# Moving the scan mixer's elementwise products from GpSimd to VectorE, and the rounding of all weights from GpSimd to ScalarE

## The chip, the cores and the metric

One core of a Trainium2 chip. TensorE (PE) multiplies matrices into PSUM, VectorE (DVE), ScalarE (ACT) and GpSimd (POOL) work on tiles of 128 partitions, and SyncE (SP) issues most of the loads. Each engine takes its instructions in the order in which the program lists them. The metric is the device time of one execution in microseconds (us), the median of several runs.

## What is computed

Two layers of a diffusion backbone over 256 context tokens and 512 latent tokens of width 1024. Each layer mixes tokens with four mixers that run side by side (a bidirectional gated recurrence with a decay per channel, called HGRN2; a bidirectional state-space scan; attention over a 2-D neighbourhood; grouped-query attention), merges them with gates, and then runs a SwiGLU network. In the reference the scan works chunk by chunk:

```python
def step(S, inp):
    qc, kc, vc, gc = inp
    b = jnp.cumsum(gc, axis=2)
    decay = jnp.exp(jnp.where(tri, b[:, :, :, None, :] - b[:, :, None, :, :], -jnp.inf))
    scores = jnp.einsum('bhtk,bhsk,bhtsk->bhts', qc, kc, decay)
    o = jnp.einsum('bhts,bhsv->bhtv', scores, vc) + jnp.einsum('bhtk,bhkv->bhtv', qc * jnp.exp(b), S)
    b_end = b[:, :, -1:, :]
    S = S * jnp.exp(b_end[:, :, 0, :])[..., None] + jnp.einsum('bhsk,bhsv->bhkv', kc * jnp.exp(b_end - b), vc)
    return S, o
```

## The kernel before

Every large product is made of three matmuls. A float32 operand is split into a rounded high part and a rest, and `mm3` (lines 240 to 246) adds high·high, high·rest and rest·high in PSUM, so a product of one 128-deep slice is the three lines L244, L245 and L246. Activations are split once per stage (the tile `h`); weights are split each time that they are loaded.

`wload` (line 205) loads one block of weights, at most 128x1056, on SP's queue into `wf` (two buffers), makes the high part `wh` on POOL (L219), and the rest `wl = wf - wh` on DVE (L220). `wh` and `wl` have four buffers each, so a block's high part can be written only once PE is done with the block four before it. `wchunk` (line 224) loads 512 or 1024 rows of some columns, one or two calls of `wload`. There are 288 blocks in the program.

The scan mixer (`hgrn`, line 537) takes 128-token tiles two at a time: three such pairs in layer 0, two in layer 1. First it makes the running sums of the log decays (`aB`, L557) and, for both directions, `aks` = key times decay to the end of the tile (L571 to L575, 128x1536), from which PE makes the states. Then for each pair it builds the scores inside a tile level by level (`LEVELS`, seven of them: distances 64, 32, ... 1). One level is: four differences of running sums on DVE (L632 to L635, 128x256 each), two exponentials on ACT (L637, 128x512), the product with the query `E[0] * q` on POOL (L638, 128x512), two products with the keys on DVE (L640, 128x256 each), 32 small matmuls of 64x64 on PE (L615), and the merge of the result into `D2` (L645 and L647 on ACT for the first two levels, L649 on DVE for the others). After the levels come the diagonal, with `kd` = sum of the keys (L651, POOL), and two products with the query for the part that comes through the states (L666, POOL). The tiles of a level are taken from a ring of eleven buffers named `s`.

PE has other work in the meantime: the gates of the merge. `gate_unit` (line 1182) loads 256 columns of the gate's weights for two units, multiplies, and ACT takes the result out of PSUM (L1190); `fill` places such units between the stages, and the ones of the scan and of both attentions run beside them. The attentions take their softmax on ACT (L922 and L925 in the grouped-query one, L977 in the other), and their scores sit in the PSUM buffers `pq` and `pl` that PE needs for the next ones.

The order of the instructions on each engine is not written out by hand: a scheduler in the tile framework goes through the program with a model of the engines' times and lists each engine's instructions in the order in which it expects them to become ready. It decides where between the other instructions a moved one comes to stand.

Of the kernel before, what the change touches and what calls it, by code (L numbers as in the profile page):

```python
# [16 lines left out]
ALU = mybir.AluOpType  # L17
# [72 lines left out]
def block_kernel(ctx, tc, t, out, dbg=None):  # L90
    nc = tc.nc
# [16 lines left out]
    def nm(s):  # L108
        uid[0] += 1
        return f"{s}_{uid[0]}"  # L110

    def pm():
        return ps.tile([P, 512], F32, tag="pm", name=nm("pm"), bufs=2)
# [4 lines left out]
    def pq():  # L118
        return ps.tile([P, 512], F32, tag="pq", name=nm("pq"), bufs=3)
# [88 lines left out]
    def wload(src, a, b):  # L208

        wf = wt.tile([P, WN], F32, tag="wf", name=nm("wf"), bufs=2)  # L210
        wh = wt.tile([P, WN], F32R, tag="wh", name=nm("wh"), bufs=4)
        wl = wt.tile([P, WN], F32R, tag="wl", name=nm("wl"), bufs=4)
        n = 0
        for s in (src if isinstance(src, list) else [src]):
            k = s.shape[-1]
            nc.sync.dma_start(wf[:, :a * b].rearrange("p (a b) -> p a b", a=a)[:, :, n:n + k], s)
            n += k
        assert n == b
        nc.gpsimd.tensor_scalar(wh[:, :a * b], wf[:, :a * b], 1.0, 0.0, op0=ALU.mult, op1=ALU.add)  # L219
        nc.vector.tensor_tensor(wl[:, :a * b], wf[:, :a * b], wh[:, :a * b].bitcast(F32), op=ALU.subtract)  # L220
        return (wh[:, :a * b].rearrange("p (a b) -> p a b", a=a),
                wl[:, :a * b].rearrange("p (a b) -> p a b", a=a))
# [216 lines left out]
    def mixing(l, h, hpool, W0):  # L439
# [9 lines left out]
        with tc.tile_pool(name=f"mx{l}", bufs=1, reuse_waits="tile") as mp:  # L449
            GB = 1552  # L450

            def g6(name, dt=F32):
                return mp.tile([P, GB], dt, tag="g", name=nm(name), bufs=12)


            def s2(shape):

                n = int(np.prod(shape[1:]))
                tl = mp.tile([P, 512], F32, tag="s", name=nm("s"), bufs=11)[:, :n]
                if len(shape) == 2:  # L460
                    return tl
                names = ["a", "b", "c", "d"][:len(shape) - 1]
                return tl.rearrange(f"p ({' '.join(names)}) -> p {' '.join(names)}", **dict(zip(names, shape[1:])))
# [4 lines left out]
            def tu(tl):  # L468
                return tl[:, :1536].rearrange("p (i u s) -> p i u s", i=6, u=2)

            def au(tl):
                return tl[:, :1536].rearrange("p (a s) -> p a s", a=12)
# [64 lines left out]
            def hgrn(q, kf, kb, v):  # L537
# [28 lines left out]
                for d, B, kk in ((0, Bf, kf), (1, Bb, kb)):  # L566
                    ks = g6("aks")
                    ksa = au(ks)
                    end = B[:, :, 128:129].to_broadcast([P, 12, P])
                    if d == 0:  # L570
                        nc.vector.tensor_tensor(ksa, end, B[:, :, 1:129], op=ALU.subtract)  # L571
                        nc.scalar.activation(ksa, ksa, AF.Exp)
                    else:
                        nc.scalar.activation(ksa, B[:, :, 0:128], AF.Exp)
                    nc.gpsimd.tensor_tensor(ksa, ksa, au(kk), op=ALU.mult)  # L575
                    order = [0, 1, 2, 3, 4] if d == 0 else [1, 0, 5, 4, 3]
                    kT = au(g6("akT"))
                    for i4 in range(3):
                        po = pm()
                        for m in range(4):  # L580
                            nc.tensor.transpose(po[:, m * P:(m + 1) * P], ksa[:, i4 * 4 + m, :], ident)
                        nc.scalar.copy(kT[:, i4 * 4:i4 * 4 + 4, :].rearrange("p a s -> p (a s)"), po)
                    St = g6("aS")
                    S4 = tu(St)
                    nc.gpsimd.memset(St[:, :1536], 0.0)
                    nxt = order[1:] + [5 if d == 0 else 2]
                    for n, i in enumerate(order):
                        po = pm()
                        for u in range(2):
                            mm(po[:, u * P:(u + 1) * P], kT[:, 2 * i + u, :], v3[:, i, u * P:(u + 1) * P], start=True, stop=True)  # L590
                        for u in range(2):
                            for hh in range(2):
                                sl = slice(hh * 64, hh * 64 + 64)
                                dst = S4[sl, nxt[n], u, sl]
                                src = po[sl, u * P + hh * 64:u * P + hh * 64 + 64]
                                if n == 0:
                                    nc.vector.tensor_copy(dst, src)
                                else:
                                    nc.vector.scalar_tensor_tensor(dst, S4[sl, i, u, sl], dec[sl, d, 2 * i + u:2 * i + u + 1],
                                                                   src, op0=ALU.mult, op1=ALU.add)  # L600
                    S.append(S4)
                o = g6("ao")
                for i2 in range(i0, TI, 2):
                    a1 = 2 * i2
# [13 lines left out]
                    def block(x, b, off=0):  # L618
                        return x[b * 64:b * 64 + 64, :, (b ^ off) * 64:(b ^ off) * 64 + 64]
                    for li, hlf in enumerate(LEVELS):  # L620
                        E = [s2([P, 4, P]) for _ in range(2)]
                        nb = 64 // hlf

                        def vw(ap):
                            return ap.rearrange("p a (n w s) -> p a n w s", w=2, s=hlf)
                        Eq, Ek = vw(E[0]), vw(E[1])
                        fi, bi = vw(Bf[:, a1:a1 + 4, 1:129]), vw(Bb[:, a1:a1 + 4, 0:128])
                        fx = vw(Bf[:, a1:a1 + 4, 0:128])
                        sh = [P, 4, nb, hlf]
                        fm, bm = fx[:, :, :, 1, 0:1].to_broadcast(sh), bi[:, :, :, 1, 0:1].to_broadcast(sh)  # L630
                        tt = nc.vector.tensor_tensor
                        tt(Eq[:, :, :, 1], fi[:, :, :, 1], fm, op=ALU.subtract)  # L632
                        tt(Eq[:, :, :, 0], bm, bi[:, :, :, 0], op=ALU.subtract)  # L633
                        tt(Ek[:, :, :, 0], fm, fi[:, :, :, 0], op=ALU.subtract)
                        tt(Ek[:, :, :, 1], bi[:, :, :, 1], bm, op=ALU.subtract)  # L635
                        for e_ in E:
                            nc.scalar.activation(e_, e_, AF.Exp)  # L637
                        nc.gpsimd.tensor_tensor(E[0], E[0], au(q)[:, a1:a1 + 4], op=ALU.mult)  # L638
                        for w_, kk in ((0, kf), (1, kb)):
                            nc.vector.tensor_tensor(Ek[:, :, :, w_], Ek[:, :, :, w_], vw(au(kk)[:, a1:a1 + 4])[:, :, :, w_], op=ALU.mult)  # L640
                        pr = scores([pm(), pm()] if li % 2 else [pq(), pq()], E[1], E[0], li == 0)
                        for hh in range(2):
                            if li == 0:
                                for b in range(2):
                                    nc.scalar.copy(block(sc[hh], b, 1), pr[hh][b * 64:b * 64 + 64])  # L645
                            elif li == 1:
                                nc.scalar.copy(D2[:, hh], pr[hh])  # L647
                            else:
                                nc.vector.copy_predicated(D2[:, hh], masks[:, li - 2:li - 1, :].to_broadcast([P, 4, 64]), pr[hh])  # L649
                    kd = s2([P, 4, P])  # L650
                    nc.gpsimd.tensor_tensor(kd, au(kf)[:, a1:a1 + 4], au(kb)[:, a1:a1 + 4], op=ALU.add)  # L651
                    pr = scores([pm(), pm()], kd, au(q)[:, a1:a1 + 4])
                    for hh in range(2):
                        nc.vector.copy_predicated(D2[:, hh], masks[:, 5:6, :].to_broadcast([P, 4, 64]), pr[hh])
# [4 lines left out]
                    for d, B in ((0, Bf), (1, Bb)):  # L659
                        e = s2([P, 4, P])  # L660
                        if d == 0:
                            nc.scalar.activation(e, B[:, a1:a1 + 4, 1:129], AF.Exp)
                        else:
                            nc.vector.tensor_tensor(e, B[:, a1:a1 + 4, 128:129].to_broadcast([P, 4, P]), B[:, a1:a1 + 4, 0:128], op=ALU.subtract)
                            nc.scalar.activation(e, e, AF.Exp)
                        nc.gpsimd.tensor_tensor(e, e, au(q)[:, a1:a1 + 4], op=ALU.mult)  # L666
                        qs.append(e)

                    for i in (i2, i2 + 1):
# [746 lines left out]
    for l in range(DEPTH):  # L1416
# [7 lines left out]
        with tc.tile_pool(name=f"ff{l}", bufs=1, reuse_waits="tile") as fp:  # L1424
# [68 lines left out]
            for pi_, (k0, nk) in enumerate(parts):  # L1493
                a = new_h(hpool)
# [82 lines left out]
```

## Time and profile before

| | before |
|---|---|
| median of 3 runs | 2589.57 us (2587.47 to 2589.83) |
| the profiled execution | 2589.94 us, of which the span of the profile is 2587.9 us |
| PE busy | 2479.7 us (96% of the span) |
| weight loads into PE (PEld) busy | 2116.2 us (82%) |
| DVE busy | 1404.5 us (54%) |
| POOL busy | 824.7 us (32%) |
| ACT busy | 556.1 us (21%) |
| TensorE's granted clock, mean | 0.987 of full |

A row of a view of the profile names the line of the kernel, the engine, the operation, and `out<-in` with the tiles' names. `x35` is a count. In a group's row the busy time and the mean duration of one instruction in ns come first, then the idle time of that engine just before these instructions and which instruction ended it. In the windows view each stretch (us from the start of the span) has its length and then the busy time of every engine, with the number of its instructions in brackets, the granted clock of TensorE as a share of full speed, the share of the DMA engines and GB/s.

### The profile page before, as it was taken

The page shows a single profiled execution, that of the slowest core. Times are in us where ns is not written, and L with a number is a line of the kernel's source. Part 1 is how long each engine was busy: PE and PEld are TensorE (multiplying, and loading weights), DVE is VectorE, ACT ScalarE, POOL GpSimd, SP SyncE. Part 2 cuts the span into 40 slices and gives each one's busy share as a digit, 9 for nine tenths or more (in the row PEclk, how much of TensorE's full clock was granted, in tenths as well). Part 3 has the DMA queues.
Part 4 walks back from the last instruction along what each step waited for, and adds up shares of the span by engine and source line. Part 5 has one row for each costly group of instructions (what it writes and reads, how often), then busy time and mean ns, then how long its engine had stood idle before and what let it go on. Part 6 is the DMA issues. An engine that isn't in the chain of part 4 may idle for free.

```text
span 2587.9 us, 41771 instructions
## 1 busy us (share of the span) xinstructions
PE 2479.7 (96%) x17088; PEld 2116.2 (82%) x17088; DVE 1404.5 (54%) x2646; ACT 556.1 (21%) x1147; POOL 824.7 (32%) x866
## 2 busy tenths in 40 slices
PE   7898899999999999999999999989999999999998
PEld 5777778889778988898998987767877678898987
DVE  4467666446447662343333464868566666443335
ACT  3233332232321141101001033224132311200010
POOL 2233343112114351111141262434223255322324
PEclk9999999999999999999999999999999999999999
DMA  7443113212226454212122164321323255433232
GB/s 244 123 148 124 47 42 89 85 58 70 90 88 210 153 165 127 73 52 64 60 64 66 58 196 136 119 79 50 102 66 107 74 185 176 123 98 98 90 97 76
DMA packets 251938, 269.56 MB, mean 104 GB/s; under 512 B 14971, under 2 KB 219875, under 8 KB 251747
## 3 DMA queue, kind: packets, MB, share of 16 engines
q1 hardware_dynamic: 236867, 238.69, 29.7%
q10 hardware_dynamic: 14880, 28.21, 3.0%
q8 instruction: 134, 2.20, 0.3%
q14 instruction: 57, 0.47, 0.1%
HBM read 238.28 MB, written 26.48 MB: 102 GB/s over the span
## 4 chain that ended last, share of the span: by engine, by line
PE 77%; DVE 10%; POOL 4%; DMA 3%; issue 3%; ACT 2%; SPq 1%; POOLq 0%; ACTq 0%; DVEq 0%
PE pl L244 16%; PE pl L246 15%; PE pl L245 15%; PE pq L245 6%; PE pq L246 6%; PE pq L244 6%; DVE wl L220 2%; DMA wa<-in_ada_w_dram 1%; PE po L311 1%; PE po L954 1%; DVE s L640 1%; DVE s L1243 1%; PE pm L942 1%; POOL wh L219 1%; DVE s L633 1%
## 5 line engine op out<-in xcount | busy, mean ns | idle before, releaser
L219 POOL TENSOR_SCALAR wh<-wf 128x1024 fp32r<-128x1024 f32 (+2 forms) x288 | 332.5, 1155 | 1084.5 <-PE pq L245 475.5
L244 PE MATMUL pl<-h,wh 128*128 128x512 f32 (+1 forms) x1720 | 625.3, 364 | 5.9 <-ACT s L925 1.9
L246 PE MATMUL pl<-h,wl 128*128 128x512 f32 (+1 forms) x1720 | 619.8, 361 | 5.4 <-DVE wl L220 5.4
L245 PE MATMUL pl<-h,wh 128*128 128x512 f32 (+1 forms) x1720 | 620.2, 361 | 0.2 <-DVE h L429 0.2
L220 DVE TENSOR_TENSOR wl<-wf,wh 128x1024 fp32r<-128x1024 f32 (+2 forms) x288 | 403.5, 1406 | 356.9 <-POOL wh L219 353.4
L244 PEld LDWEIGHTS pl<-h,wh 128*128 128x128 f32 x1720 | 327.5, 190 | 71.6 <-issue 17.8
L246 PEld LDWEIGHTS pl<-h,wl 128*128 128x128 f32 x1720 | 327.5, 190 | 61.7 <-issue 8.7
L245 PEld LDWEIGHTS pl<-h,wh 128*128 128x128 f32 x1720 | 327.2, 190 | 51.6 <-issue 7.1
L244 PE MATMUL pl<-wh,h 128*128 128x256 f32 (+1 forms) x1048 | 298.4, 285 | 3.7 <-DVE tmpo L1263 2.2
L245 PE MATMUL pl<-wl,h 128*128 128x256 f32 (+1 forms) x1048 | 297.5, 284 | 1.5 <-DVE wl L220 1.5
L246 PE MATMUL pl<-wh,h 128*128 128x256 f32 (+1 forms) x1048 | 297.1, 284 | 0.0
L244 PE MATMUL pq<-h,wh 128*128 128x256 f32 (+1 forms) x680 | 219.3, 323 | 1.1 <-POOL wh L219 1.1
L246 PE MATMUL pq<-h,wl 128*128 128x256 f32 (+1 forms) x680 | 218.7, 322 | 0.6 <-DVE wl L220 0.6
L245 PE MATMUL pq<-h,wh 128*128 128x256 f32 (+1 forms) x680 | 218.2, 321 | 0.0
L244 PEld LDWEIGHTS pl<-wh,h 128*128 128x128 f32 x1048 | 199.0, 190 | 9.3 <-DVE tmpo L1263 3.7
L245 PEld LDWEIGHTS pl<-wl,h 128*128 128x128 f32 x1048 | 198.8, 190 | 6.4 <-issue 4.0
L246 PEld LDWEIGHTS pl<-wh,h 128*128 128x128 f32 x1048 | 199.1, 190 | 3.2 <-issue 2.9
L245 PE MATMUL pq<-wl,h 128*128 128x256 f32 x600 | 169.1, 282 | 0.0
L244 PE MATMUL pq<-wh,h 128*128 128x256 f32 x600 | 169.0, 282 | 0.0
L246 PE MATMUL pq<-wh,h 128*128 128x256 f32 x600 | 169.0, 282 | 0.0
L244 PEld LDWEIGHTS pq<-h,wh 128*128 128x128 f32 x680 | 127.9, 188 | 15.4 <-issue 2.5
L245 PEld LDWEIGHTS pq<-h,wh 128*128 128x128 f32 x680 | 128.1, 188 | 12.4 <-issue 0.7
(420 smaller groups left out, 3798.1 us busy)
## 6 DMA issues: line engine op xcount, KB each, us to landing
wf<-in_w_in_dram SPq DMA_DIRECT2D x120, 512.0 KB, 3.7
wa<-in_ada_w_dram SPq DMA_DIRECT2D x96, 512.0 KB, 3.9
wf<-in_ffn_w_up_dram SPq DMA_DIRECT2D x176, 256.0 KB, 3.1
wf<-in_ffn_w_down_dram SPq DMA_DIRECT2D x32, 512.0 KB, 3.3
gsp<-gs ACTq DMA_DIRECT2D x32, 384.0 KB, 2.9
gld<-gsp SPq DMA_DIRECT2D x16, 768.0 KB, 4.6
wf<-in_w_branch_dram SPq DMA_DIRECT2D x16, 512.0 KB, 3.3
wf<-in_w_out_dram SPq DMA_DIRECT2D x16, 512.0 KB, 3.3
```

Of the source, the lines that this page charges most:

```text
L219: nc.gpsimd.tensor_scalar(wh[:, :a * b], wf[:, :a * b], 1.0, 0.0, op0=ALU.mult, op1=ALU.add)
L220: nc.vector.tensor_tensor(wl[:, :a * b], wf[:, :a * b], wh[:, :a * b].bitcast(F32), op=ALU.subtract)
L244: mm(po, ah, bh, start=(k == 0), stop=False)
L245: mm(po, ah, bl, start=False, stop=False)
L246: mm(po, al, bh, start=False, stop=(k == n - 1))
L311: mm(po[32 * j:32 * j + 32, :], cT[:, k].rearrange("p r s -> p (r s)"), wf[:, j * 256:(j + 1) * 256], start=(k == 0), stop=(k == KT - 1))
L633: tt(Eq[:, :, :, 0], bm, bi[:, :, :, 0], op=ALU.subtract)
L640: nc.vector.tensor_tensor(Ek[:, :, :, w_], Ek[:, :, :, w_], vw(au(kk)[:, a1:a1 + 4])[:, :, :, w_], op=ALU.mult)
L942: nc.tensor.transpose(pt[:, (2 * k + j) * P:(2 * k + j + 1) * P], x, ident)
L954: mm(po[hh * 64:hh * 64 + 64, :], va(hh, k), PT[hh][k], start=(k == 0), stop=(k == nk - 1))
L1243: nc.vector.scalar_tensor_tensor(tq, sg[:, n % 2, g[0]:g[1]], 1.0, po, op0=ALU.add, op1=ALU.mult)
```

## The change

Three kinds of instruction leave POOL. The rounding of a weight block to its high part (L219, 288 times) goes to ACT, as a copy. The scan mixer's products and sums L575 (4 times, 128x1536), L638 (35 times), L651 (5 times) and L666 (10 times, all 128x512) go to DVE. What is computed stays the same, and so do the loads and the number of buffers. POOL keeps the additions of the merge and the residuals, the small steps of the norms, the rounding of activations, and its part in the state-space scan and the attentions.

```diff
@@ wload
-        nc.gpsimd.tensor_scalar(wh[:, :a * b], wf[:, :a * b], 1.0, 0.0, op0=ALU.mult, op1=ALU.add)
+        nc.scalar.copy(wh[:, :a * b], wf[:, :a * b])
         nc.vector.tensor_tensor(wl[:, :a * b], wf[:, :a * b], wh[:, :a * b].bitcast(F32), op=ALU.subtract)
@@ hgrn
-                    nc.gpsimd.tensor_tensor(ksa, ksa, au(kk), op=ALU.mult)
+                    nc.vector.tensor_tensor(ksa, ksa, au(kk), op=ALU.mult)
...
-                        nc.gpsimd.tensor_tensor(E[0], E[0], au(q)[:, a1:a1 + 4], op=ALU.mult)
+                        tt(E[0], E[0], au(q)[:, a1:a1 + 4], op=ALU.mult)
...
-                    nc.gpsimd.tensor_tensor(kd, au(kf)[:, a1:a1 + 4], au(kb)[:, a1:a1 + 4], op=ALU.add)
+                    nc.vector.tensor_tensor(kd, au(kf)[:, a1:a1 + 4], au(kb)[:, a1:a1 + 4], op=ALU.add)
...
-                        nc.gpsimd.tensor_tensor(e, e, au(q)[:, a1:a1 + 4], op=ALU.mult)
+                        nc.vector.tensor_tensor(e, e, au(q)[:, a1:a1 + 4], op=ALU.mult)
```

The scheduler places the moved instructions. On DVE, in the first pair of tiles of layer 0's scan (the tiles `s` are the levels' operands, `aB` the running sums, `aq`, `akf`, `akb` query and keys, `wl` the rest of a weight block), a piece of the difference between the two orders:

```order
 L634 TENSOR_TENSOR s_1389<-aB_1103 128x64x4
 L635 TENSOR_TENSOR s_1389<-aB_1120 128x64x4
-L220 TENSOR_TENSOR wl_2449<-wf_2447,wh_2448 128x1024
+L638 TENSOR_TENSOR s_1326<-s_1326,aq_612 128x512
 L632 TENSOR_TENSOR s_1419<-aB_1103 128x128x2
 L633 TENSOR_TENSOR s_1419<-aB_1120 128x128x2
 L634 TENSOR_TENSOR s_1420<-aB_1103 128x128x2
 L635 TENSOR_TENSOR s_1420<-aB_1120 128x128x2
+L220 TENSOR_TENSOR wl_2449<-wf_2447,wh_2448 128x1024
 L640 TENSOR_TENSOR s_1327<-s_1327,akf_613 128x16x16
 L640 TENSOR_TENSOR s_1327<-s_1327,akb_614 128x16x16
+L638 TENSOR_TENSOR s_1357<-s_1357,aq_612 128x512
```

The product with the query, which was not on this engine, now stands between the differences of a later level and the products with the keys.

On ACT, in layer 1's grouped-query attention (`ats` and `atm` are the softmax's sums and maxima, `pq`, `pl`, `pm` PSUM buffers, `gs` a gate unit's result on its way out of PSUM):

```order
 L922 ACTIVATE s_19022,ats_19019<-pq_19016,atm_19018 128x256
 L925 ACTIVATE s_19054,ats_19019<-pq_19046,atm_19018 128x512
+L219 CAST wh_19440<-wf_19439 128x1024
 L947 COPY s_18895<-pm_18949 128x512
 L925 ACTIVATE s_19060,ats_19021<-pl_19047,atm_19020 128x512
+L219 CAST wh_19446<-wf_19445 128x1024
 L1190 ACTIVATE gs_19125<-pl_19126 128x512
 L1191 DMA gsp_14512<-gs_19125 128x512
```

The two roundings of a gate block now stand between an exponential of one score block, the copy of the transposed probabilities (L947) and the next exponential, and ahead of the gate unit that is the last one to read the block four before.

## Rows read from the trace of the kernel before

**Rows 1.** The page's part 1: busy time, share of the span and instructions of each engine.
```profile
PE 2479.7 (96%) x17088; PEld 2116.2 (82%) x17088; DVE 1404.5 (54%) x2646; ACT 556.1 (21%) x1147; POOL 824.7 (32%) x866
```
**Rows 2.** Windows: scan, attentions (layer 0); scan, attentions, start of the merge (layer 1).
```profile
97.00:291.00 194.00, 170.74 (x1709) 137.14 (x1709) 138.94 (x267) 65.02 (x125) 74.18 (x60) 0.92 0.37 121
455.00:777.00 322.00, 319.40 (x2023) 261.22 (x2022) 163.41 (x444) 86.23 (x242) 65.06 (x82) 1.00 0.24 78
1585.00:1747.00 162.00, 144.49 (x1234) 118.74 (x1233) 117.88 (x214) 51.58 (x97) 66.38 (x50) 0.97 0.32 101
1844.00:2070.00 226.00, 219.74 (x1304) 172.05 (x1303) 144.91 (x395) 64.28 (x173) 60.21 (x65) 0.98 0.27 85
2102.00:2167.00 65.00, 61.41 (x339) 52.48 (x339) 49.95 (x63) 8.66 (x14) 47.24 (x32) 0.97 0.68 220
```
**Rows 3.** Waits of PE over the whole span: us in total, times, longest.
```profile
PE pq L615 <- DVE s L640: 14.2, 8, 4.4
...
PE pq L615 <- DVE s L649: 10.1, 4, 4.7
PE pq L1168 <- ACT s L925: 6.3, 3, 3.9
...
PE pm L615 <- DVE s L649: 4.8, 3, 2.8
```
**Rows 4.** Timeline of DVE in layer 0's scan: start, duration (us), instruction.
```profile
257.75 0.42 DVE L632 TENSOR_TENSOR s<-aB 128x256 f32<-128x256 f32 x1
258.09 1.54 DVE L633 TENSOR_TENSOR s<-aB 128x256 f32<-128x256 f32 x1
```
**Rows 5.** Timeline of POOL in the same stretch.
```profile
257.92 1.43 POOL L638 TENSOR_TENSOR s<-s,aq 128x512 f32<-128x512 f32 x1 [2.68 <-ACT s L637]
```
**Rows 6.** DVE's groups by shape: the levels' two-input instructions.
```profile
L640 DVE TENSOR_TENSOR s<-s,akb 128x256 f32<-128x256 f32 x35 | 30.4, 869 | 0.0
L640 DVE TENSOR_TENSOR s<-s,akf 128x256 f32<-128x256 f32 x35 | 29.0, 828 | 17.5 <-ACT s L637 17.3
...
L633 DVE TENSOR_TENSOR s<-aB 128x256 f32<-128x256 f32 x35 | 27.3, 781 | 0.0
...
L632 DVE TENSOR_TENSOR s<-aB 128x256 f32<-128x256 f32 x35 | 21.8, 623 | 2.0 <-PE pm L615 2.0
```
**Rows 7.** DVE's groups by shape: two inputs of 512 and of 1536 elements.
```profile
L854 DVE TENSOR_TENSOR s<-s,s 128x512 f32<-128x512 f32 x10 | 6.9, 688 | 4.0 <-ACT s L853 3.9
...
L571 DVE TENSOR_TENSOR aks<-aB 128x1536 f32<-128x1536 f32 x2 | 3.5, 1730 | 0.0
```
**Rows 8.** POOL's groups by shape: two of the scan's products.
```profile
L638 POOL TENSOR_TENSOR s<-s,aq 128x512 f32<-128x512 f32 x35 | 52.2, 1495 | 52.2 <-ACT s L637 46.3 <-issue 5.8
...
L575 POOL TENSOR_TENSOR aks<-aks,akf 128x1536 f32<-128x1536 f32 x2 | 8.8, 4395 | 8.9 <-ACT aks L572 8.9
```
**Rows 9.** The weights' rest on DVE: its group, and its durations (min/median/max, ns).
```profile
L220 DVE TENSOR_TENSOR wl<-wf,wh 128x1024 fp32r<-128x1024 f32 (+2 forms) x288 | 403.5, 1406 | 356.9 <-POOL wh L219 353.4
...
L220 DVE TENSOR_TENSOR wl<-wf,wh x288: 941/1226/4449, 19.3 to 2559.5; 128x1024 fp32r<-128x1024 f32 x142, 128x1056 fp32r<-128x1056 f32 x2
```
**Rows 10.** What POOL waited for ahead of the weights' rounding L219 (us, times).
```profile
  PE pq L245: 475.5, 88
```
**Rows 11.** ACT's groups by shape: the roundings that it does before, two sizes.
```profile
L1509 ACT CAST h<-sg 128x512 fp32r<-128x512 f32 x40 | 24.8, 621 | 232.6 <-DVE sg L1507 232.6
...
L1509 ACT CAST h<-sg 128x256 fp32r<-128x256 f32 x30 | 12.1, 407 | 83.8 <-DVE sg L1507 83.8
```
**Rows 12.** Windows of line L219 alone: length, POOL's busy time and count, clock, DMA.
```profile
97.00:291.00 194.00, 16.63 (x14) 0.92 0.37 121
455.00:777.00 322.00, 29.01 (x26) 1.00 0.24 78
1585.00:1747.00 162.00, 20.33 (x18) 0.97 0.32 101
1844.00:2070.00 226.00, 28.70 (x24) 0.98 0.27 85
```

## The prediction

> **What bounds the kernel now.** I read the busy shares first. PE is busy for 2479.7 us of a span of 2587.9 us and no other engine comes near [rows 1], so whatever this change saves or costs has to show in the 108.2 us in which PE stands still, or in TensorE's clock. None of the moved instructions is on PE, and relief for POOL, busy a third of the span, is no gain by itself.
>
> So the next view is the windows, cut by stage: where does PE stand still? In the two scan stretches it loses 194.0 - 170.7 = 23.3 us (layer 0) and 162.0 - 144.5 = 17.5 us (layer 1), 40.8 us together; in the attentions 2.6 + 6.3 = 8.9 us; at the start of layer 1's merge 3.6 us [rows 2]. The same rows show the granted clock: 0.92 and 0.97 in the scans, 1.00 in layer 0's attentions (1.00 is 2.4 GHz; a mean below it says that a part of the stretch ran at 1.2 GHz). Against full speed that is 0.08 x 194 = 15.5 us and 0.03 x 162 = 4.9 us, 20.4 us in all, and it is lost in the stretches where PE pauses and then runs small matmuls.
>
> The third view is what PE waits for. The scan's small matmuls wait 14.2 + 10.1 + 4.8 = 29.1 us for DVE, for the products with the keys and for the merge of a level's scores [rows 3]. DVE is the late one there: it is busy 139 of 194 us and 118 of 162 us [rows 2].
>
> The fourth view is the timeline inside a level, and it is what this prediction rests on. A difference of running sums takes 0.42 us; the next one, equal in size, takes 1.54 us, and just then POOL runs its product of 1.43 us that began at 257.92 us [rows 4, 5]. It ends at 259.63 us, 0.28 us after POOL's end at 259.35. The reader should see that DVE's "busy" time in the scan is partly time in which it stands behind POOL. The groups show the size of it: equal instructions average 869, 828, 781 and 623 ns in place of 420 [rows 6].
>
> **The change, part by part.** The sum is made against the profiled execution's own 2589.9 us, which is 0.4 us above the median of the three runs.
>
> *Products onto DVE (scan).* Added: 35 + 10 + 5 = 50 of 128x512. The nearest row on DVE with two inputs is 0.688 us [rows 7], so 34.4 us. Removed: with POOL's product gone, the four groups of 35 fall to about 420 ns: 35 x (449 + 408 + 361 + 203) ns = 49.7 us [rows 4, 6]. The four products of 128x1536 go from 4.40 us on POOL to 1.73 us on DVE [rows 7, 8]. During such a POOL product DVE's two-input work stands anyway, so I count the two for which rows show the price, 2 x 2.67 = 5.3 us, and leave the other two at zero.
>
> *Rounding onto ACT, as DVE sees it.* The rest `wl` averages 1.406 us against a median of 1.226 [rows 9]; in the scans there are 14 + 18 = 32 blocks [rows 12], so 32 x 0.18 = 5.8 us less. In the other stages this saves DVE time that PE does not wait for.
>
> DVE's chain in the two scans becomes 34.4 - 49.7 - 5.3 - 5.8 = -26.4 us, that is shorter. What of it does PE get? At most all 26.4; if only the part of PE's idle time counts that names this chain, 29.1 of 40.8, it is 18.8. I take 22, between them, because the gate units that fill PE cannot also be late. The clock's 20.4 us should come back in the same share, 22 / 40.8, which is 11 us. No row shows how the clock answers to fewer pauses; the ends are 0 and 20.4 us.
>
> *Rounding onto ACT, as ACT sees it.* From 621 ns for 512 and 407 ns for 256 elements, ACT adds 214 ns per 256, so a block of 1024 costs it 0.621 + 2 x 0.214 = 1.05 us [rows 11]. For 288 blocks that is some 300 us, and ACT goes from 556 to about 856 us, a third of the span. By throughput that is covered. The covers that could break are two. In the scans ACT's exponentials stand between DVE's differences and the products: 32 blocks x 1.05 = 33.6 us if each delayed the chain, 0 if none did. ACT is busy 65 of 194 us there [rows 2] and several levels are in flight, so I count one block in eight, 4 us. In the attentions there are 26 + 24 = 50 blocks, in 25 pairs [rows 12]: 52.5 us if each of them held PE, 0 if none did. The nearest row is PE's own wait for an exponential there, 6.3 us in three waits [rows 3]; one more block in each of the three is 3.2 us, which I take.
>
> What is queued behind a waiting rounding matters more than its length. POOL waited 475.5 us in 88 places, 5.4 us each, for PE to finish with an older block [rows 10]. On POOL almost nothing stood behind it. On ACT the copy of the probabilities and the next exponential do, as the second piece of the order shows. On SP's queue only a few loads swap places with a neighbour, and a `wf` buffer is given back when the rest is made, so the loads come about when they came.
>
> *Merge.* At its start POOL is busy 47 of 65 us and DVE 50, and PE loses 3.6 us [rows 2]. POOL's roundings go away there: between 0 and 3.6 us, I take 2. The start, the norms and the end keep their POOL steps, and I count nothing.
>
> Sum: -22 - 11 + 4 + 3.2 - 2 = -27.8 us, so 2589.9 - 27.8 = 2562.1; for the median that is **2562 us**. The terms' own ends (18.8, no clock and the ACT costs doubled; 26.4, all of the clock and no ACT cost; the merge's 2 in both) put this case between 2583 and 2541 us.
>
> The Trainium skill, in Perfetto Trace Analysis, section Optimizing Scalar/DVE Operations, says that GpSimd and DVE share an SBUF read port, "so offloading operations between those two might not help". The trace agrees on the sharing (the 1.54 us beside the 1.43 us), but the rule taken as a verdict speaks against moving the products at all. By it the scan would stay as it is and the time would be that of the third rival below.
>
> **The rivals.**
>
> *More than that.* The whole idle time of the scans vanishes with the clock's loss and the merge's: 40.8 + 20.4 + 3.6 = 64.8 us, 2525 us. For it: all the waits named for the scan's matmuls are for DVE [rows 3], and nothing that PE does in the scans is added. Against it: DVE stays busy for two thirds of the scan, and its exponentials now share ACT with roundings. Chance 0.16.
>
> *Slower: roundings hold up the attention.* Place: ACT in both attentions, where a rounding that waits for PE stands ahead of an exponential whose scores hold a PSUM buffer. Price: if each of the 25 pairs costs PE the pair's own 2.1 us, that is 52.5 in place of 3.2 us, and 2562 + 49 = 2611 us. It decides from (27.8 + 3.2) / 25 = 1.24 us of PE per pair on. For it: the 5.4 us waits and the new order. Against it: the scheduler lists by expected readiness, PE has gate units to run, and PE loses only 8.9 us in 548 us of attention now. Chance 0.14.
>
> *No change: one queue's delay for another's.* The roundings stand ahead of the scan's exponentials so often (33.6 us at most) that they eat the 26.4 us; merge and attention leave -2 + 3.2, 2591 us. Against it is ACT's low share. Chance 0.13.
>
> *The change does not do what it says.* DVE's long instructions have another cause, so that DVE gets 34.4 + 4 x 1.73 = 41.3 us and loses nothing; in the share 29.1 / 40.8 PE loses 29 us more, 2619 us. Rows 4 and 5 speak plainly against it. Chance 0.02.
>
> **How the numbers follow.** The forecast has the rest, 0.55, and its own range is 2541 to 2583. A measurement of this kernel can tell 0.2% (5.2 us) from no change, so faster means below 2584.4 and slower above 2594.8. Faster: 0.55 + 0.16 and 0.02 of the third rival's spread, 0.73. Slower: 0.14 + 0.02 and 0.01 of that spread, 0.17. The same: 0.10. For 8 in 10 the range goes from 2535 (it leaves out half of the first rival, 0.08) to 2594 (it leaves out most of the slower cases, 0.12).
>
> **What would show it.** Right: in the scan stretches the levels' L632, L633 and L640 average near 420 ns, L638 on DVE near 0.69 us, PE's waits of L615 for DVE fall from 29 us to under 10, the clock there rises above 0.95, and L220 averages near 1.23 us everywhere. The roundings on ACT take 1.05 us. Wrong: L633 or L640 stay above 600 ns (then POOL was not the cause); PE's waits for L925, L922 or L977 grow beyond 20 us (the slower rival); waits of the scan's PE matmuls name ACT's L637 (the no-change rival). The prediction fails as a whole if PE's idle time in the two scans does not fall by at least a quarter.

## The result, and the profile after

The changed kernel takes 2549.66 us (median of four runs, 2548.04 to 2552.92), the kernel before on the same chip 2589.70 us (2587.47 to 2590.23). The ratio is 0.985, with a 95% interval of 0.9836 to 0.9864. That is 40 us less, where 28 were forecast; the time lies in the forecast's own range of 2541 to 2583. The profiled execution has a span of 2548.6 us, 39.3 us less than before.

The page's part 1 of the changed kernel:

```profile
PE 2475.3 (97%) x17088; PEld 2114.5 (83%) x17088; DVE 1315.8 (52%) x2700; ACT 842.7 (33%) x1437; POOL 393.2 (15%) x524
```

Against [rows 1]: PE runs the same 17088 matmuls and stands still for 73.3 us in place of 108.2. DVE has 54 instructions more and is busy 88.7 us less. That is the first thing to see: work was added to an engine, and its busy time fell.

DVE's groups by shape, the levels' instructions (mean ns after the comma):

```profile
L638 DVE TENSOR_TENSOR s<-s,aq 128x512 f32<-128x512 f32 x35 | 24.0, 685 | 7.8 <-ACT s L637 7.7
...
L633 DVE TENSOR_TENSOR s<-aB 128x256 f32<-128x256 f32 x35 | 15.1, 430 | 0.0
L632 DVE TENSOR_TENSOR s<-aB 128x256 f32<-128x256 f32 x35 | 15.0, 427 | 4.1 <-PE pm L615 3.1 <-PE pm L676 1.0
...
L640 DVE TENSOR_TENSOR s<-s,akf 128x256 f32<-128x256 f32 x35 | 14.7, 419 | 1.0 <-ACT s L637 1.0
L640 DVE TENSOR_TENSOR s<-s,akb 128x256 f32<-128x256 f32 x35 | 14.7, 419 | 0.0
...
L575 DVE TENSOR_TENSOR aks<-aks,akb 128x1536 f32<-128x1536 f32 x2 | 3.5, 1753 | 2.3 <-ACT aks L574 2.3
```

The four groups of [rows 6] are at 419 to 430 ns, the level of the one undisturbed instruction in [rows 4]. The product with the query costs 0.685 us on DVE where it cost 1.495 on POOL [rows 8], and L575 1.75 where it cost 4.40.

PE's waits over the whole span:

```profile
PE pq L1168 <- ACT s L925: 7.6, 3, 3.9
...
PE pm L615 <- DVE s L649: 4.4, 3, 3.4
...
PE pq L615 <- DVE s L640: 3.1, 2, 1.6
```

The scan's small matmuls wait 7.5 us for DVE, where it was 29.1 in the rows shown [rows 3] (30.8 with a wait of 1.7 us for L640 that stands further down in that view).

The same work moves to other times, so stretches are compared between the same instructions in both kernels. For the two scans the windows go from L557 to L808 (a transposition of the state-space scan): in layer 0 from the first of the one to the first of the other, in layer 1 from the last to the last. Before:

```profile
105.00:321.00 216.00, 192.74 (x1806) 155.10 (x1805) 150.64 (x280) 74.31 (x139) 80.07 (x70) 0.93 0.32 104
1606.00:1792.00 186.00, 169.47 (x1326) 139.93 (x1326) 143.84 (x221) 64.70 (x115) 81.70 (x71) 0.97 0.29 91
```

and after:

```profile
102.00:299.00 197.00, 187.24 (x1805) 150.70 (x1804) 135.06 (x313) 91.15 (x156) 10.60 (x24) 0.97 0.36 115
1584.00:1756.00 172.00, 168.99 (x1328) 138.92 (x1327) 125.74 (x244) 84.71 (x135) 13.12 (x26) 0.99 0.32 99
```

PE does the same number of matmuls, but for one, in 369 us in place of 402. Of the 33 us, 27 are idle time (39.8 to 12.8) and 6 are busy time, with a higher granted clock. Elsewhere, from the first instruction of a stage to the first of the next: 3.2 us less before the first scan, 6.2 us more in layer 0's grouped-query attention (208.5 to 214.7 us, L1110 to L1243), 2.8 less in its merge and output product (L1243 to L1505), 3.6 less from there to the last L557 of layer 1, 0.6 less in layer 1's grouped-query attention, 2.6 less in its merge and output product, and 0.2 or less in every other stage. That makes 39.3.

The weights' rounding and rest, from part 5 of the page:

```profile
L220 DVE TENSOR_TENSOR wl<-wf,wh 128x1024 fp32r<-128x1024 f32 (+2 forms) x288 | 368.6, 1284 | 347.0 <-ACT wh L219 346.2
L219 ACT CAST wh<-wf 128x1024 fp32r<-128x1024 f32 (+2 forms) x288 | 298.6, 1037 | 529.3 <-PE pq L246 233.9
```

The rounding waits for PE on ACT as it did on POOL [rows 10]: ACT stands idle 529.3 us ahead of these instructions, most of it for PE, and in most stages this costs nothing. The rest is at 1284 ns, 122 less than in [rows 9].

### The profile page after: what moved, and what is told of

Its sections match the earlier page's. It is cut to its first block, busy times and chain, and to the rows that moved or that the text cites. A ratio compares the mean times of both kernels' runs of the same rounds, so it can differ in the third digit from the quotient of the medians.

```text
span 2548.6 us, 41600 instructions
## 1 busy us (share of the span) xinstructions
PE 2475.3 (97%) x17088; PEld 2114.5 (83%) x17088; DVE 1315.8 (52%) x2700; ACT 842.7 (33%) x1437; POOL 393.2 (15%) x524
## 4 chain that ended last, share of the span: by engine, by line
PE 84%; DVE 6%; DMA 3%; POOL 2%; ACT 2%; issue 2%; SPq 1%; POOLq 0%; ACTq 0%; DVEq 0%
PE pl L244 17%; PE pl L245 17%; PE pl L246 17%; PE pq L244 7%; PE pq L245 7%; PE pq L246 7%; DMA wa<-in_ada_w_dram 2%; PE po L311 1%; PE po L954 1%; DVE wl L220 1%; PE pm L942 1%; PE pq L1168 1%; DVE s L1243 1%; PE po L1001 1%; PE pq L1072 1%
## 5 line engine op out<-in xcount | busy, mean ns | idle before, releaser
L220 DVE TENSOR_TENSOR wl<-wf,wh 128x1024 fp32r<-128x1024 f32 (+2 forms) x288 | 368.6, 1284 | 347.0 <-ACT wh L219 346.2
L219 ACT CAST wh<-wf 128x1024 fp32r<-128x1024 f32 (+2 forms) x288 | 298.6, 1037 | 529.3 <-PE pq L246 233.9
L1267 POOL TENSOR_TENSOR x<-x,tmpo 128x256 f32<-128x256 f32 x100 | 90.3, 904 | 895.6 <-DVE tmpo L1263 885.0
L245 PEld LDWEIGHTS pq<-h,wh 128*128 128x128 f32 x680 | 128.6, 189 | 14.3 <-issue 1.9
```

The source lines that it names most:

```text
L219: nc.scalar.copy(wh[:, :a * b], wf[:, :a * b])
L245: mm(po, ah, bl, start=False, stop=False)
L1267: nc.gpsimd.tensor_tensor(X[t_][:, cs], X[t_][:, cs], tmp, op=ALU.add)
```

## The experiments

Theory: an instruction of DVE with two inputs stands still while POOL reads, so the work taken from POOL gives DVE more than it costs. Rivals: the gain is the rounding's alone, or the new order's.

**Each half alone.** First the products on DVE, with the rounding left on POOL:

```diff
-        nc.scalar.copy(wh[:, :a * b], wf[:, :a * b])
+        nc.gpsimd.tensor_scalar(wh[:, :a * b], wf[:, :a * b], 1.0, 0.0, op0=ALU.mult, op1=ALU.add)
```

> Only the scan's products move to DVE; the weights are still rounded by POOL. Theory A (in the scan POOL's products stop DVE, and that is most of the gain): the prediction's own terms for the products, 34.4 - 49.7 - 5.3 = -20.6 us of DVE's chain, of which PE gets about 17 with about 8 us of clock: 2564 us, between 2558 and 2572. DVE's L633 and L640 fall below 550 ns on average but not to 420, since POOL's roundings still fall among them. Rival B (most of the gain comes from the roundings that leave POOL): 2580 us or more.

Measured: 2562.98 us (2560.89 to 2569.88) against 2589.13, ratio 0.9902 (0.9886 to 0.9919). Then the rounding on ACT, with the products left on POOL (the kernel before with the first line of the change alone):

> Only the rounding of the weights moves to ACT; the scan's products stay on POOL. Theory A: the changed kernel gained 40 us and the products alone should give about 25, so 15 are left: 2575 us, between 2568 and 2586. L220 falls to about 1.25 us outside the scans; L633 and L640 stay near 800 ns inside them. Rival B: 2565 us or less, and the two parts alone sum to the 40 us with the larger share here.

Measured: 2576.91 us (2571.14 to 2579.37), ratio 0.9946 (0.9929 to 0.9962). The halves give 26.2 and 12.2 us, together 38.4 of the 40. DVE's groups show how they share the stall. With POOL's rounding only (the first kernel; its L633 averages 460 ns):

```profile
L634 DVE TENSOR_TENSOR s<-aB 128x256 f32<-128x256 f32 x35 | 17.1, 489 | 0.2 <-PE pm L676 0.2
...
L640 DVE TENSOR_TENSOR s<-s,akf 128x256 f32<-128x256 f32 x35 | 15.5, 444 | 0.8 <-ACT s L637 0.7
```

With POOL's products only (the second; its L633 averages 523 ns, where the expectation had about 800):

```profile
L638 POOL TENSOR_TENSOR s<-s,aq 128x512 f32<-128x512 f32 x35 | 74.7, 2150 | 109.8 <-ACT s L637 99.8 <-PE pl L246 5.2 <-PE pm L679 4.7
...
L640 DVE TENSOR_TENSOR s<-s,akf 128x256 f32<-128x256 f32 x35 | 28.5, 815 | 11.0 <-ACT s L637 10.7
L640 DVE TENSOR_TENSOR s<-s,akb 128x256 f32<-128x256 f32 x35 | 24.4, 696 | 0.0
L632 DVE TENSOR_TENSOR s<-aB 128x256 f32<-128x256 f32 x35 | 20.6, 588 | 1.2 <-PE pm L615 1.2
```

Most of the stall is the products', as forecast, and a smaller part the rounding's. The stall goes both ways, and the mean of 2150 ns hides how (shortest, median and longest in ns):

```profile
L638 POOL TENSOR_TENSOR s<-s,aq x35: 1268/1470/7785, 119.6 to 1712.1; 128x512 f32<-128x512 f32 x35
```

The median is 1470 ns, but four of the 35 products take 5.9 to 7.8 us. Each of these four stands beside 12 to 20 of DVE's two-input instructions that run back to back at their usual length, 0.42 us for 128x256, and it ends 1.15 to 1.18 us after the last of them.

**POOL's reading, put back.** The changed kernel, where POOL makes one more product of the same size in each level, into a tile that nobody reads:

```diff
+                        xt_ = s2([P, 4, P])
+                        nc.gpsimd.tensor_tensor(xt_, E[0], au(q)[:, a1:a1 + 4], op=ALU.mult)
```

> The changed kernel, and beside each of the 35 products on DVE POOL makes the same product once more into a tile of the ring that nobody reads. Nothing waits for it except the ring of eleven buffers. Theory A (POOL at work stops DVE's two-input instructions): DVE stands some 1.1 us in each level again, 35 x 1.1 = 38 us, and also does the products itself: the gain of the products is lost and more, 2575 to 2605 us, L633 or L640 averaging over 600 ns. Rival C (the product is simply sooner done on DVE, 0.69 in place of 1.43 us, and nothing stands): 2550 us, at most 2556, with L633 and L640 near 420 ns.

and, in its place, work for POOL of about the same length that reads nothing:

```diff
+                        xt_ = s2([P, 4, P])
+                        for _ in range(3):
+                            nc.gpsimd.memset(xt_, 0.0)
```

> As the run with the unused product, but POOL only fills that tile with zeros, three times per level, so that it is busy about as long (a fill of 1536 elements took 1.38 us) and the ring is as full, but reads nothing. If what stops DVE is that POOL reads from the same memory, this costs only what the fuller ring costs: 2550 to 2562 us, L633 and L640 near 420 ns. If any work on POOL stops DVE, it costs as much as the unused product. The difference of the two runs is the price of POOL's reading; the difference of this one to the changed kernel (2550) is the ring's.

Measured: 2560.82 us (2559.09 to 2569.54) with the product and 2541.55 (2535.01 to 2543.95) with the memsets. The first lies between the ranges of its theory and its rival: a part of the products' gain is lost, 11 us, not all of it. The second is under its range. DVE's products with the keys and differences with the unread product:

```profile
L642 DVE TENSOR_TENSOR s<-s,akb 128x256 f32<-128x256 f32 x35 | 30.5, 871 | 0.0
...
L642 DVE TENSOR_TENSOR s<-s,akf 128x256 f32<-128x256 f32 x35 | 20.6, 590 | 0.2 <-ACT s L637 0.2
...
L632 DVE TENSOR_TENSOR s<-aB 128x256 f32<-128x256 f32 x35 | 16.4, 468 | 0.1
```

and with the memsets:

```profile
L641 POOL MEMSET s<- 128x512 f32 x105 | 53.1, 524 | 165.8 <-PE pq L615 150.6 <-PE pm L682 5.3 <-PE pm L679 5.3
...
L632 DVE TENSOR_TENSOR s<-aB 128x256 f32<-128x256 f32 x35 | 15.0, 429 | 9.0 <-PE pm L615 6.4 <-PE pm L679 2.4
...
L643 DVE TENSOR_TENSOR s<-s,akf 128x256 f32<-128x256 f32 x35 | 14.8, 422 | 1.6 <-ACT s L637 1.5
L643 DVE TENSOR_TENSOR s<-s,akb 128x256 f32<-128x256 f32 x35 | 14.7, 421 | 0.0
```

The group that runs just after POOL's start pays: 871 ns with reads, 421 with writes of the same size. The two engines' timelines laid side by side say the same of every kernel. Of the levels' 210 instructions of 128x256 on DVE (L632 to L635 and L640 in the kernel before), so many take over 0.5 us, and so much longer than 0.42 us do the 210 take together:

```
kernel                               over 0.5 us   over 0.42 us each, together
before                                   62            51.9 us
products on DVE alone                    18             6.3
rounding on ACT alone                    45            40.2
changed, product nobody reads            35            25.0
changed, three memsets per level         12             2.2
changed                                   7             1.1
```

Every one of the long ones overlaps an instruction of POOL that reads: a product, a rounding or, in all of the last two rows, a copy of a score block (L656). In the memset kernel 48 instructions run beside a memset and nothing else of POOL, and none of them takes over 0.5 us. So it is POOL's reading that stops DVE, not POOL being busy. The 19 us between the two kernels are not all the stall's, though, since their orders differ (below). The Trainium skill, in SBUF — State Buffer, section SBUF: two separate sides, says that a DVE instruction with two SBUF inputs contends only against a GpSimd instruction that reads SBUF. These two runs agree with it. That the memsets would be 8 us faster than the changed kernel itself was not expected. Two questions were left: these 8 us, and the 6 us lost in layer 0's attention.

**The attention's roundings, back on POOL.** A flag is true while the program's text is in the 2-D and the grouped-query attention of a layer and in the gate units that are left after them (the lines that set it are not shown):

```diff
-        nc.scalar.copy(wh[:, :a * b], wf[:, :a * b])
+        if att[0]:
+            nc.gpsimd.tensor_scalar(wh[:, :a * b], wf[:, :a * b], 1.0, 0.0, op0=ALU.mult, op1=ALU.add)
+        else:
+            nc.scalar.copy(wh[:, :a * b], wf[:, :a * b])
```

> The changed kernel, but the blocks loaded while the two attention stages of a layer run are rounded on POOL again. Theory (there ACT's 1.05 us roundings stand ahead of the exponentials and copies that TensorE waits for: layer 0's second attention took 214 us with them and 208 without): that stretch goes back to 208 us, TensorE's wait for L925 goes, and the time falls to about 2544 (2541 to 2547). Rival (the 6 us come from the order of the matmuls or a short fall of the clock, not from ACT): 2548 to 2553, the stretch still 214 us.

Measured: 2547.33 us (2544.48 to 2549.73), ratio 0.984 (0.982 to 0.9861). Layer 0's grouped-query attention in the changed kernel and then in this one:

```profile
555.00:770.00 215.00, 211.46 (x1306) 171.77 (x1305) 101.38 (x267) 72.85 (x177) 22.97 (x38) 0.98 0.24 81
```
```profile
554.00:763.00 209.00, 206.59 (x1304) 168.76 (x1301) 103.77 (x267) 58.26 (x162) 39.33 (x52) 1.00 0.25 83
```

The stretch is 6 us shorter and its clock is back at 1.00; PE's longest wait for L925 there falls from 2.4 to 1.0 us. So the roundings on ACT do cost that stretch 6 us, 5 of them in PE's busy time (211.5 to 206.6), that is through the clock. Every other pair of kernels that differ in these roundings shows it: 208.5 to 214.3 us (before, and the rounding alone on ACT), 208.4 to 214.7 (the products alone, and the changed kernel), and, in runs that follow, 213.8 to 219.3 (ring of 7) and 209.2 to 214.8 (three memsets). The median of this run is just above its expected range and only 2.3 us under the changed kernel, with intervals that overlap; in the two pairs that follow the medians differ by 6.2 and 7.3 us.

**The order.** In the memset kernel it is the end of layer 0's scan that is shorter. In the changed kernel's timeline of PE these three waits stand there:

```profile
253.83 0.68 PE L615 MATMUL pm<-s,s 64*64 64x64 f32 x26 [0.30 <-DVE s L649]
256.02 0.69 PE L615 MATMUL pq<-s,s 64*64 64x64 f32 x32 [1.51 <-DVE s L640]
260.09 1.46 PE L615 MATMUL pm<-aq,s 64*64 64x64 f32 x32 [3.38 <-DVE s L649]
```

What differs there is the order in which the scheduler lists PE's matmuls. Between the products of the last levels of that scan it lists so many other matmuls, by which PE can cover DVE's part of a level (a matmul in plain f32, as the scan's own are, has two records in the trace and counts once here):

```
kernel                                     other matmuls between the last level products
before                                     44  59  18   5
changed                                    48  59   4   5
changed, three memsets per level           50  50   9   1  24
changed, ring of 7                         35  48  10  33  37
changed, score copies on ACT               52  62  18  30
```

The next runs test whether the order is what counts. The first takes a ring `s` of 7 tiles in place of 11, in the changed kernel (`bufs=11` becomes `bufs=7`):

> The changed kernel with a ring of 7 scratch tiles in place of 11, nothing else. Theory (what is left of TensorE's waits in the scans is where the order puts several level products with 2 to 8 matmuls of other work between them, so that DVE's four subtractions and products of a level are not covered; a ring of 7 spreads the products, with 28 to 50 other matmuls between): the 9.8 us of idle TensorE in layer 0's scan (97 to 291 us) fall below 4, the clock there rises from 0.97 to 0.99 or more, and the time falls to about 2541 (2536 to 2546). Rival (a level then waits for buffers of the one before, and DVE falls behind): TensorE waits more for L638, L640 and L649, 2553 to 2575.

Measured: 2556.17 us (2554.95 to 2559.3), slower, and in the rival's range. The waits of DVE in its first scan hold a new one:

```profile
DVE s L632 <- PE pm L676: 9.9, 2, 6.2
```

The next pair's first difference has no tile until PE has read the last pair's. PE's waits of L615 for DVE grow from 7.5 to 17.9 us, the longest 5.2 us for one L640. But the stages show that the loss is not in layer 0's scan (lengths in us: in layer 0 from the first L557 to the first L1110 and from there to the first L1243, in layer 1 from the first L557 to the first L1243; the last two rows belong to the runs that follow):

```
kernel                       layer 0: scan to         layer 0: grouped-    layer 1: scan to end of
                             end of 2-D attention     query attention      grouped-query attention
before                       471.4                    208.5                500.5
changed                      452.9                    214.7                484.1
changed, ring of 7           446.5                    219.3                491.2
before, ring of 7            463.6                    214.7                505.6
changed, ring of 7, att.     447.8                    213.8                491.7
```

In the first column the ring of 7 is 6.4 us better, with the same count of matmuls but for two, 15 us of idle PE in both and a higher clock. It loses 4.6 us in layer 0's grouped-query attention, which takes its tiles from the same ring, and 7.1 in layer 1. The theory's own signs, less than 4 us of idle PE from 97 to 291 us and a clock of 0.99, did not come (12.5 us and 0.97). The same ring in the kernel before:

> The kernel before the change with a ring of 7 scratch tiles. Theory (the change took time out of DVE's chain, the order is another matter, but the two overlap since wider gaps also cover a blocked DVE): 2574 to 2584, DVE's L640 still 600 to 850 ns. Rival (the change gained through the order of TensorE's work, which a ring of 7 gives as well): 2545 to 2562, within 10 us of the ring of 7 in the changed kernel.

Measured: 2591.87 us (2587.82 to 2595.31), ratio 1.001 (0.9998 to 1.0021): nothing in all, above the ranges of both theory and rival. By stages it is again a gain of 7.8 us in the first column and a loss in the other two, with L640 still at 829 and 936 ns. The change gains 18.5 in the first column, so its gain is not had by this order. Both edits together, the ring of 7 and the attention's roundings on POOL, in the changed kernel:

> The ring of 7 and the roundings on POOL in the attention stages, both in the changed kernel. If the two effects are in different stretches, their gains add: about 2535 (2529 to 2541). If each only frees time that the other takes back, no better than the better one alone.

Measured: 2549.94 us (2549.23 to 2553.53), 6.2 us under the ring of 7 alone. The attention's edit gains with either ring; the sum that was expected failed with the ring's part of it.

Then one memset per level in place of three (`range(3)` becomes a single call). The scheduler lists PE's work of that scan as in the changed kernel:

> The changed kernel with one memset, by POOL, of an unread ring tile per level (three before: 2541.6). In layer 0's scan TensorE's instructions stand as in the changed kernel, while the buffers turn as with the three memsets. Theory (the three memsets gained because the scheduler, which costed them, put other matmuls between the last levels of that scan, where the changed kernel's TensorE idles 5.2 us of 246 to 268 us at a clock of 0.84): that idle time is there again, and the layer's first gated-norm stage begins as in the changed kernel, at about 410 us, total 2546 to 2554. Rival (the tiles that turn faster, or POOL's writes, do it): idle time gone, that stage begins at about 402 us, 2539 to 2544.

Measured: 2554.72 us (2551.78 to 2555.71), no faster than the changed kernel. What follows layer 0's state-space scan (L1030, for the 2-D attention) starts at 411.8 us, in the changed kernel at 410.5 and with three memsets at 401.9. The windows of 246 to 268 us, in the changed kernel, with one memset, and with three:

```profile
246.00:268.00 22.00, 16.82 (x251) 13.84 (x249) 14.31 (x38) 8.16 (x11) 2.46 (x4) 0.84 0.18 45
```
```profile
246.00:268.00 22.00, 16.82 (x253) 14.06 (x253) 14.96 (x41) 8.55 (x12) 3.66 (x6) 0.84 0.14 44
```
```profile
246.00:268.00 22.00, 22.00 (x294) 17.68 (x293) 14.99 (x40) 9.09 (x14) 4.67 (x10) 1.00 0.26 86
```

The same listing gives the same 5.2 us of idle PE and the same clock of 0.84, memset or not. So the gain there goes with the listing, through idle time and clock, and not with a memset in each level or with tiles that turn faster.

**What is fastest.** The three memsets and the attention's roundings on POOL in one:

> Both that have been faster than the changed kernel, in one: three memsets of an unread tile per level, and the roundings on POOL while the attention stages run. The first gained 8 us in layer 0's scan and gated norm, the second 2 to 6 in the attention's stretch; different stretches, so 2537 (2533 to 2540). If the order of the scans, which is another than in either, loses its gain: 2543 to 2549.

Measured: 2534.27 us (2532.38 to 2538.04), in the expected range: 15.4 us under the changed kernel, where the two edits alone gave 8.1 and 2.3. And a way to such a listing without idle work: the kernel of the attention's roundings, with the score blocks' copies on ACT:

```diff
-                            nc.gpsimd.tensor_copy(block(sc[hh], b), D2[b * 64:b * 64 + 64, hh])
+                            nc.scalar.copy(block(sc[hh], b), D2[b * 64:b * 64 + 64, hh])
```

> The changed kernel with the roundings on POOL in the attention stages, and with the eight copies of score blocks per pass of the scans moved from POOL to ACT (POOL then has nothing in a pass that reads beside DVE), no unread tiles. The order then has 18 to 62 other matmuls between the last levels of layer 0's scan, in place of 4 and 5. Theory (order decides): idle time at the end of that scan gone, the scan and gated norm 6 to 8 us shorter than in the same kernel with the copies on POOL (2547.3): 2537 to 2543. Rival (ACT, which has the exponentials and the roundings too, now holds up the levels; or the copies on POOL cost nothing and the order little): 2545 to 2560.

Measured: 2529.24 us (2528.4 to 2532.99), ratio 0.9769 (0.9755 to 0.9784): the fastest, 20 us under the changed kernel, and below the range of its theory. Its window there, and a stretch of its scan in layer 1:

```profile
246.00:268.00 22.00, 22.00 (x307) 18.43 (x306) 13.79 (x38) 10.36 (x19) 0.00 (x0) 1.00 0.26 86
...
1566.00:1726.00 160.00, 159.31 (x1270) 131.07 (x1269) 117.44 (x238) 83.06 (x135) 3.30 (x12) 1.00 0.33 100
```

Against the kernel with the copies on POOL the median is 18 us lower, of which the profiled spans show 12.7 (2543.9 to 2531.2). The copies (four per pass, not the eight that the expectation says) were also reads of POOL beside DVE, 20 of 506 ns in the changed kernel. In the kernel with the copies on POOL they lengthen ten instructions of DVE, by 1.5 us together. And the kernel with the three memsets and the attention's roundings on POOL, which has its copies on POOL too, needs 517.7 us for its two scans (from the first L557 to the first L1030), against 516.5 here and 529.6 with the copies on POOL and no memsets. So most of the gain goes with the listing; no run changes the listing alone. Last, the same edit in the kernel before:

> The kernel before the change with one edit: the copies of score blocks on ACT in place of POOL. In the changed kernel with POOL's attention roundings that edit gave 18 us (2547.3 to 2529.2). Theory (in the kernel before, DVE's own chain, with 600 to 850 ns for each blocked operation, bounds the levels, so that a better order of TensorE's work has little to gain until that chain is shorter): 2580 to 2590, and the changed split is worth more at the better order (over 50 us) than at the old one (40). Rival (the two gains are independent): 2568 to 2575.

Measured: 2583.92 us (2581.36 to 2587.78), ratio 0.9978 (0.9968 to 0.9987), 5 us. DVE's products there are as long as ever:

```profile
L640 DVE TENSOR_TENSOR s<-s,akf 128x256 f32<-128x256 f32 x35 | 31.5, 899 | 22.6 <-ACT s L637 22.4
L640 DVE TENSOR_TENSOR s<-s,akb 128x256 f32<-128x256 f32 x35 | 27.6, 789 | 0.0
```

The time is in the theory's range, but the run does not test the theory: PE's trace has 18 and 5 other matmuls between the last level products, as in the kernel before, so the edit did not bring the better listing there. Whether that listing would help a DVE with these stalls stays open; the ring of 7 gave 7.8 us in the first column above with them. With the copies on ACT in both kernels, the change with the attention's roundings on POOL is worth 54.7 us (2583.9 to 2529.2), and this includes the listing that came with it.

## Why the prediction was right, point by point

The mechanism was right: DVE stood behind POOL's reads, and taking POOL's products away made DVE's chain shorter although it got 54 instructions more. Each sign that was to show it is there but one: the levels' instructions are at 419 to 430 ns, the product at 0.685, PE's L615 waits 7.5 us for DVE, the clock in the scans is 0.97 and 0.99, a rounding takes ACT 1.05 us. The exception is L220, whose mean is 1.28 and not 1.23 us: its median is 1.225, as before, but the longest still take 2.33 us (4.45 before). POOL's other reads remain: 35 of the 288 take over 1.3 us, each beside an instruction of POOL, and of the 19.6 us that they lose 13.4 stand beside the merge's additions (L1245) and 4.5 beside those of the residuals (L1267). No run took these away.

- *Products onto DVE.* Added 24.0 + 6.8 + 3.4 = 34.2 us (L638, L666, L651), forecast 34.4. Removed in the four groups: 108.5 to 59.5 us, 49.0, forecast 49.7. But the forecast gave all of this to POOL's products. In the trace before, about 42.5 of the 49.7 us stand beside the products that the change moved (26.8 beside L638, 7.3 beside L666, 5.1 beside L575, 3.3 beside L651), 6.7 beside the roundings and 0.9 beside the score copies.
- *The rest of DVE's chain* came out near its sum by errors that made up for each other, which is luck. The term for L575 (-5.3 us) had the wrong sign: the four products add 7.0 us to DVE, and the stall that they caused while they were on POOL, 5.1 us in two of the levels' instructions, was already in the 49.7. Against that the rest L220 fell by 11.9 us in the two windows, where 5.8 were counted, and other instructions (L664, L634 and smaller ones) by some 9 that were not counted. By the durations added up DVE lost 28.7 us where the terms made 26.4; by busy time, in which neighbours that overlap count once, 33.7 (294.5 to 260.8).
- *What PE gets of it.* Idle time fell by 27.0 us, where 22 were taken between 18.8 and 26.4. The clock gave 6.0 us of PE's busy time where 11 of 20.4 were taken. The sum, 33, came out as forecast; its two parts did not, and that their errors cancel is luck too.
- *ACT in the scans*, taken as 4 us, cost nothing that shows: no wait of PE's scan matmuls names L637. That it cost nothing at all was not tested.
- *Attention.* Taken as 3.2 us for both layers. It is 6.2 in layer 0's grouped-query attention and a gain of 0.6 in layer 1's. The step that failed here is the count by PE's waits alone: those grew by 1.3 us (6.3 to 7.6), while the clock of that stretch fell from 1.00 to 0.98.
- *Merge*, taken as 2 us: 2.8 us in layer 0's merge and output product and 2.6 in layer 1's. At the start, and between the layers, where nothing was counted, 3.2 and 3.6 us were gained. In the SwiGLU network DVE's L1510 fell from 1025 to 689 ns. That this is what gained the 3.6 us was not shown.

So the difference to the forecast (39.3 in place of 27.8 us) is 4 from the scans, where the 4 us of ACT do not show, 6.8 from the start and the stretch between the layers, 3.4 from the two merges, less 2.4 in the attentions (6.2 - 0.6 in place of 3.2) and 0.3 in other stages.

The rivals: the slower one named the right engine and place, but its price was 6 us in one layer and not 52.5. The better one (2525 us, all idle time and clock of the scans and the merge's idle time) was not reached by the change. The kernel with the score copies on ACT and the attention's roundings on POOL comes to 2529.

## What to carry to other kernels

Before moving work between GpSimd and VectorE, look in VectorE's timeline for equal instructions of unequal length, and at what GpSimd reads just then: busy time can be waiting time, and work moved onto the engine can shorten it. When an off-path engine gets a long instruction, look at PE's clock in the stretches that it serves, not at PE's waits alone: here a wait that grew by 1.4 us came with a stretch that grew by 6. After such a move, count what stands between the dependent matmuls in the new order: here the kernel with 18 and 30 matmuls there was 18 us faster than the one with 4 and 5, and most of that goes with the listing. And when a shared ring of buffers is made smaller, look at every stage that takes tiles from it: the gain in one scan was lost in the attentions.

## What was not expected of the hardware

A memset of 128x512 by GpSimd (524 ns) leaves VectorE's two-input instructions at 421 to 437 ns, while a product of the same size beside them stretches one group to 871. And the stall is mutual: in the kernel where only the rounding was moved, one product of GpSimd took 7.8 us in place of 1.3 to 1.5, while 20 two-input instructions of VectorE ran back to back beside it.
